# A mixture-of-experts stage: second blocks of up to 64 rows in two products instead of three, and weight splits spread over nine places

## The chip, the core and the metric

The kernel runs on one core of a Trainium2 chip. The metric is the device time of one execution in microseconds (us). A core has TensorE (PE, matrix products out of SBUF into PSUM, with PEld for its weight loads), VectorE (DVE), ScalarE (ACT), GpSimd (POOL) and SyncE (SP), and 16 DMA engines. The engines run side by side, each in the order of its own instructions, and wait for one another through semaphores.

## The reference

One encoder layer on 2048 tokens of width 1024, all in float32: windowed attention and a two-way mLSTM, gated and projected, and then a mixture of 32 experts, each token in two of them. The change is in the experts alone:

```python
xs = xt[row_tok].reshape(nblk, MOE_BLOCK, D)          # rows of an expert, in blocks of 128

def expert_block(args):
    xb, e = args
    return (jax.nn.silu(xb @ w_gate[e]) * (xb @ w_up[e])) @ w_down[e]

ys = lax.map(expert_block, (xs, blk_e)).reshape(P, D)
y = jnp.zeros((T, D), ys.dtype).at[row_tok].add(ys * row_w[:, None].astype(ys.dtype))
```

`w_gate` and `w_up` are 1024 x 512 and `w_down` 512 x 1024 for each expert, so an expert has 6.3 MB of weights. Counted with the reference's own routing on its inputs, the 32 experts get between 89 and 180 rows. 15 of them have more than 128: experts 1, 7, 8, 10, 11, 14 to 17, 19, 20 and 27 to 30. The fullest second block has 52 rows.

## The kernel before

Everything ahead of the experts (projections, attention, mLSTM, routing) is left alone by the change. The experts' stage is the end of `_body`, lines 1519 to 1776; its loop over the experts starts at line 1721.

**How a product keeps float32.** A float32 matrix is split into two parts that TensorE multiplies: `hi`, the rounded value (ACT writes it), and `lo`, what is left (a subtraction on DVE or POOL). A product x w is then three products into one PSUM bank: x_hi w_hi, x_lo w_hi, x_hi w_lo. Rows are the 128-column stationary side, weights the 512-column moving side.

**Weights.** An expert's weights are 12 pieces: 8 row blocks of gate and up (`raw`), 4 of down (`rawd`), two pieces to a loaded tile of 1 MB, six of these at a time (`NRAW`, SP issues the loads). `wsplit(n)` splits a piece: `ehi` on ACT (L1560), `elo` on DVE, or on POOL for the pieces in `POOL_J` (L1562). Split pieces lie in a ring of 14, so 2 pieces of the next expert can be split before this one is done. Where splits stand in each engine's order is set by hand, by `SPLITS`: six pieces at place 0 (the start of the expert), the others at four later places.

**A block.** `Block` does up to 128 rows. `head` makes 48 products with gate and up (L1615 with `ehi`, L1618 with `elo`; two halves of the columns, h = 0 and 1, with 24 each), silu and product of a half (L1627 on ACT, L1628 on DVE), transposes it (L1634) and splits it (L1635, L1636). The 24 products with down (L1644, L1645, L1649) are half in `head`, half in `tail`; then the result is scaled (`y`, L1703 on ACT, L1704 on DVE) and POOL adds it to the output rows with an indirect DMA (L1705). `xturn` transposes and splits the rows (L1589 on PE, L1590, L1591), for the next expert's block behind this one's `head`.

**Second blocks.** `nb` holds the number of blocks of each expert. In a branch at the top of the loop (L1725) POOL gathers the second block's 128 rows (`xgB`, L1726). In a branch behind the first block's `head` (L1745) a second `Block` does all of it again, 72 products in three passes, with no split of a weight between its products; without a second block only the first one's `tail` stands there. On the way without it, POOL makes up for the skipped DMA with a semaphore instruction (INC_SWDGE_SEM) in either branch.

Of the kernel before, what the change touches and what calls it, by code (L numbers as in the profile page):

```python
# [20 lines left out]
P = 128  # L21
S = 2048
# [18 lines left out]
def bucket_table():  # L41
    """Relative position to bucket, as one-hot rows, and the window's mask as a last row."""
# [12 lines left out]
class Chains:  # L55
    """Queues of generators, each advanced a step at a time between blocks of matrix products."""
# [55 lines left out]
def _body(tc, nc, A, out, scr_ext, upto, es):  # L112
# [68 lines left out]
    # gates of the mLSTM, all tokens: [i|f] x tile x (dir, head)  # L181
# [12 lines left out]
    def rstd(dst, ssq, n, cnt, scale=1.0):  # L194
        """scale * (ssq / cnt + eps) ** -0.5 on GpSimd, the scale a power of two"""
# [5 lines left out]
    PW = 272  # L201

    class Stream:
# [9 lines left out]
        def dma(self, n):  # L213
            """load half n % 2 of piece n // 2"""
# [70 lines left out]
    # order of the column pieces in a chunk of tokens  # L285
# [30 lines left out]
    def run_mms(mms, nsub=6):  # L316
        """mms: list of (out, lhsT, rhs, start, stop); chains advance between sub-blocks."""
# [11 lines left out]
    # ================= first half: projections, attention, forward mLSTM =================  # L329
# [19 lines left out]
    def small_loads():  # L349
# [7 lines left out]
        # per-channel vectors: conv taps (5), conv bias, merge biases, all halved  # L357
# [6 lines left out]
    def setup():  # L364
        """attention bias [query, head, key], per-channel columns, empty slots"""
# [26 lines left out]
        # a row of zeros past the tokens, weight 0  # L392
# [21 lines left out]
    # ---- rms norm and transposition of a tile of x  # L414
# [33 lines left out]
    # ---- attention  # L448
# [133 lines left out]
    # ---- mLSTM  # L582
    def gprep(c, d, seed=False):
        """stabiliser and decay of direction d for the tiles of chunk c"""
# [61 lines left out]
    def mload(t, d):  # L646
        """a tile's q and v; forward its k, backward what the forward pass left: k by rows and k q"""
# [15 lines left out]
    def mhead(n, t, d):  # L663
        """what a tile of the recurrence does without the state, at most a tile ahead of it"""
# [48 lines left out]
    def mtile(n, t, d):  # L713
        """one tile of the recurrence"""
# [71 lines left out]
    def mpost(n, t, h_):  # L786
        """both directions joined, normed and gated"""
# [32 lines left out]
    # ---- convolution over time, silu  # L820
# [17 lines left out]
    def conv_tail():  # L838
        """the last two tokens, with zeros behind them"""
# [957 lines left out]
```

## Time and profile before

| | |
|---|---|
| device time, 3 runs | median 2782.31 us (2769.46 to 2784.45) |
| span of the profiled execution | 2774.9 us |
| experts' stage, first to last product | 1784.8 to 2763.7 us of the span: 978.9 us |
| TensorE clock granted, whole span | 0.971 of full speed |
| second blocks executed | 15 |

The page gives the span of the profiled execution and no other time for it; it lies between the fastest run and the median. A row of the timeline has the start, the duration, the engine, the line, the operation, output <- input, how many were merged, and in brackets how long the engine was idle before it and what ended that. A product's duration includes the way through the array and overlaps the next one's, so the spacing of starts is what counts. Of a group of instructions the row has the busy time and mean duration in ns, and after the second bar the idle time before them with what ended it.

### The profile page before, as it was taken

To read this page: it belongs to the slowest core of one execution; us is meant where nothing else is said; L and a number is where in the kernel's file an instruction comes from. 1 tells how busy PE (TensorE), PEld (TensorE's weight loads), DVE (VectorE), ACT (ScalarE), POOL (GpSimd) and SP (SyncE) were. 2 spreads that over 40 slices of the span, in tenths; PEclk is the share of its full clock that TensorE was granted. 3 is DMA by queue.
4 is the path that set the end of the run, shared out by engine and by line. 5 is a ranking of instruction groups with operands and counts; after the bars stand their busy time and mean duration, and the time that the engine had idled before them with its cause. 6 is when DMAs were issued, how large, how long until landed. Compare 5 with 4: busy or idle time off the path is not lost. (4 is left out here: it accounts for less than half of the span.)

```text
span 2774.9 us, 39144 instructions
## 1 busy us (share of the span) xinstructions
PE 2562.3 (92%) x14112; PEld 2129.0 (77%) x14113; DVE 1556.6 (56%) x2537; ACT 1283.7 (46%) x2500; POOL 1243.0 (45%) x1029
## 2 busy tenths in 40 slices
PE   7999999999999999978998989799999999988997
PEld 6778977897789787757977878677777777766775
DVE  4454445454545645558594937667454544567544
ACT  4444545454445444433332422357553544556543
POOL 5444444244433442324444445357643543545433
PEclk9999999999999999989999999899999999999998
DMA  5534434453345345477765644679876876779763
GB/s 159 156 113 149 135 111 121 141 160 107 114 137 161 114 127 164 148 195 213 230 199 179 186 152 127 223 252 344 283 257 191 297 242 195 266 232 324 267 194 109
DMA packets 348967, 518.68 MB, mean 187 GB/s; under 512 B 24747, under 2 KB 212228, under 8 KB 348748
## 3 DMA queue, kind: packets, MB, share of 16 engines
q1 hardware_dynamic: 332140, 460.03, 50.9%
q0 software_dynamic: 15440, 51.60, 7.9%
q10 hardware_dynamic: 1168, 4.21, 0.4%
q8 instruction: 126, 2.06, 0.3%
q14 instruction: 93, 0.76, 0.1%
HBM read 420.30 MB, written 95.47 MB: 186 GB/s over the span
## 5 line engine op out<-in xcount | busy, mean ns | idle before, releaser
L239 POOL TENSOR_TENSOR wlo<-wraw,whi 128x512 fp32r<-128x512 f32 (+1 forms) x422 | 572.7, 1386 | 472.4 <-ACT whi L236 454.4
L1618 PE MATMUL mm<-elo,xhi 128*128 128x512 f32 x752 | 276.2, 419 | 87.1 <-DVE elo L1562 50.5
L1562 DVE TENSOR_TENSOR elo<-raw,ehi 128x1024 fp32r<-128x1024 f32 x192 | 297.2, 1589 | 39.8 <-ACT ehi L1560 36.0
L1615 PE MATMUL mm<-ehi,xhi 128*128 128x512 f32 x752 | 307.6, 409 | 0.0
L319 PE MATMUL mm<-hThi,whi 128*128 128x512 f32 x768 | 306.9, 400 | 0.0
L319 PE MATMUL mm<-hTlo,whi 128*128 128x512 f32 x768 | 304.4, 396 | 0.0
L319 PE MATMUL mm<-hThi,wlo 128*128 128x512 f32 x768 | 304.0, 396 | 0.0
L1615 PE MATMUL mm<-ehi,xlo 128*128 128x512 f32 x752 | 302.4, 402 | 1.3 <-issue 1.3
L236 ACT ACTIVATE whi<-wraw 128x512 fp32r<-128x512 f32 (+1 forms) x424 | 233.4, 622 | 136.9 <-PE mm L319 59.1
L319 PE MATMUL mm<-whi,hThi 128*128 128x256 f32 (+1 forms) x896 | 260.3, 291 | 3.9 <-ACT ev L898 1.8
L319 PE MATMUL mm<-wlo,hThi 128*128 128x256 f32 (+1 forms) x896 | 256.0, 286 | 1.1 <-POOL wlo L239 1.1
L319 PE MATMUL mm<-whi,hTlo 128*128 128x256 f32 (+1 forms) x896 | 255.8, 285 | 0.0
L1618 PEld LDWEIGHTS mm<-elo,xhi 128*128 128x128 f32 x752 | 146.9, 198 | 139.8 <-DVE elo L1562 64.3
L1560 ACT ACTIVATE ehi<-raw 128x1024 fp32r<-128x1024 f32 x256 | 253.0, 1048 | 1.7 <-issue 0.5
L1705 POOL DMA_INDIRECT out<-y,idx x47 | 102.3, 2176 | 263.4 <-ACT ehi L1560 237.9
L1562 POOL TENSOR_TENSOR elo<-raw,ehi 128x1024 fp32r<-128x1024 f32 x64 | 156.4, 2444 | 127.9 <-ACT ehi L1560 127.2
L1562 POOL TENSOR_TENSOR elo<-rawd,ehi 128x1024 fp32r<-128x1024 f32 x64 | 163.9, 2560 | 79.0 <-ACT ehi L1560 79.0
L319 PEld LDWEIGHTS mm<-whi,hThi 128*128 128x128 f32 x896 | 170.2, 190 | 7.9 <-ACT ev L898 2.1
L319 PEld LDWEIGHTS mm<-wlo,hThi 128*128 128x128 f32 x896 | 170.3, 190 | 3.6 <-issue 1.6
L1615 PEld LDWEIGHTS mm<-ehi,xlo 128*128 128x128 f32 x752 | 147.5, 196 | 30.5 <-DVE xlo L1591 0.4
L319 PEld LDWEIGHTS mm<-hThi,wlo 128*128 128x128 f32 x768 | 144.3, 188 | 34.0 <-issue 3.2
L319 PEld LDWEIGHTS mm<-whi,hTlo 128*128 128x128 f32 x896 | 170.0, 190 | 0.3 <-DVE hTlo L444 0.2
(421 smaller groups left out, 5872.6 us busy)
## 6 DMA issues: line engine op xcount, KB each, us to landing
wraw<-w_in SPq DMA_DIRECT2D x152, 512.0 KB
raw<-w_expert_gate SPq DMA_DIRECT2D x128, 512.0 KB
raw<-w_expert_up SPq DMA_DIRECT2D x128, 512.0 KB
rawd<-w_expert_down SPq DMA_DIRECT2D x64, 1024.0 KB
mg_s<-evg SPq DMA_DIRECT2D x64, 256.0 KB
gt<-mg_s SPq DMA_DIRECT2D x32, 512.0 KB
wraw<-w_out SPq DMA_DIRECT2D x32, 512.0 KB
xt<-x SPq DMA_DIRECT2D x16, 512.0 KB
```

Of the source, the lines that this page charges most:

```text
L236: nc.scalar.activation(hi[:, ks, :W], r[:, k:k + 2, :W], AF.Copy)
L239: eng.tensor_sub(lo[:, ks, :W], r[:, k:k + 2, :W], hi[:, ks, :W].bitcast(F32))
L319: nc.tensor.matmul(o, l, r, start=st, stop=sp)
L1560: nc.scalar.activation(dst[0], src, AF.Copy)
L1562: eng.tensor_tensor(dst[1], src, dst[0].bitcast(F32), op=OP.subtract)
L1615: nc.tensor.matmul(self.gu[h], x_[:, k, :], self.wt(k)[0][:, h, :], start=k == 0 and i == 0, stop=False)
L1618: nc.tensor.matmul(self.gu[h], self.xs[0][:, k, :], self.wt(k)[1][:, h, :], start=False, stop=stop)
L1705: nc.gpsimd.indirect_dma_start(out=out, out_offset=bass.IndirectOffsetOnAxis(ap=self.idx, axis=0), in_=y, in_offset=None, compute_op=OP.add)
```

## The change

- A second block of up to 64 rows goes to a new class `Small`. Its rows' two parts stand side by side as one stationary tile of 128 columns (`xs`: 64 of hi, 64 of lo), which is multiplied with `ehi` and with `elo` of each piece: 2 products where there were 3. Rows 0 to 63 of the sum are then the part of x_hi, rows 64 to 127 that of x_lo. `fold` adds the two halves by a product with `sel` (two identities over each other), which transposes at the same time; behind the product with down, ACT and DVE add the halves, POOL scales (L1734) and issues the indirect DMA (L1735).
- The second block is in two short branches in the middle of the first block: transposition and the products with gate and up between `begin` and `after` (L1791); fold and the products with down beside `end` (L1798).
- Its gather has 64 rows, stands outside any branch and is made for every expert, one expert ahead.
- The splits stand at nine places. Five pieces (before: two) are split ahead of an expert's first product; `POOL_J` is (2, 5, 8, 11) instead of (1, 5, 8, 10).
- The first block's gate and up products go by pairs of pieces and halves; the rows' parts are four tiles of half the depth, so that a product waits for its half.
- An expert with over 192 rows would have all blocks but the first in the loop at the end, with its weights loaded anew; `nb` and `two` are counted for that.

The rest of the diff takes out comments and renames helpers of `Block` (`head` is now `begin`, `middle`, `after`; `tail` is `end`).

```diff
-    nc.vector.tensor_scalar(nbf, cnt[0:1, :], 127.0, None, op0=OP.add)
+    nc.vector.tensor_scalar(nbf, cnt[0:1, :], 192.0, None, op0=OP.is_gt)
+    nc.vector.scalar_tensor_tensor(nbf, cnt[0:1, :], 127.0, nbf, op0=OP.add, op1=OP.mult)
...
         def up(self, h, k0, k1):
             for k in range(k0, k1):
-                self.up_x(h, k)
-                self.up_w(h, k, k == KT - 1)
+                for i, x_ in enumerate(self.xs[k // 4]):
+                    nc.tensor.matmul(self.gu[h], x_[:, k % 4, :], self.wt(k)[0][:, h, :],
+                                     start=k == 0 and i == 0, stop=False)
+            for k in range(k0, k1):
+                nc.tensor.matmul(self.gu[h], self.xs[k // 4][0][:, k % 4, :], self.wt(k)[1][:, h, :],
+                                 start=False, stop=k == KT - 1)
...
+        def begin(self, at):
+            for i, (h, k) in enumerate(((0, 0), (1, 0), (0, 2), (1, 2), (0, 4), (0, 6))):
+                at(f"p{i}")
+                self.up(h, k, k + 2)
+            self.room()
+            self.act(0)
+            at("a0")
+            self.a0 = self.a
+            self.turned()
+            self.room()
+        def middle(self):
+            self.up(1, 4, 7)
+            self.turn(0, self.a0)
+            self.up(1, 7, KT)
+            self.act(1)
+        def after(self, at):
+            at("a1")
+            self.down(0, (0, 1))
+            at("d0")
+            self.down(1, (0, 1))
+            at("d1")
+            self.turn(1, self.a)
+            at("t1")
...
+    class Small:
+        def __init__(self, wt, xg, idx_c, wgt_c):
+            self.wt, self.xg, self.idx, self.wgt = wt, xg, idx_c, wgt_c
+            self.xs = mo.tile([P, KT, 2, 64], F32R, name="xs")
+            self.hs = mo.tile([P, 4, 2, 64], F32R, name="hs")
+            self.g = mo.tile([P, 2, 512], F32, name="g")
+            self.a = mo.tile([P, 2, 2, 64], F32, name="sa")
+            self.p = mp.tile([P, KT, 64], F32, name="tr", bufs=2)
+            self.ps = [mp.tile([P, 512], F32, name="mm", tag=f"a{h}B") for h in range(2)]
+        def turn(self):
+            for k in range(KT):
+                nc.tensor.transpose(self.p[:, k, :], self.xg[0:64, k * P:(k + 1) * P], ident[0:64, 0:64])
+            nc.scalar.activation(self.xs[:, :, 0, :], self.p, AF.Copy)
+            nc.vector.tensor_sub(self.xs[:, :, 1, :], self.p, self.xs[:, :, 0, :].bitcast(F32))
+        def product(self, h, lhs, w, k, n):
+            for m in range(2):
+                nc.tensor.matmul(self.ps[h], lhs[:, k].rearrange("p a t -> p (a t)"), w[m][:, h, :],
+                                 start=k == 0 and m == 0, stop=k == n - 1 and m == 1)
+        def up(self):
+            for h in range(2):
+                for k in range(KT):
+                    self.product(h, self.xs, self.wt(k), k, KT)
+                if h == 0:
+                    nc.scalar.activation(self.g[:, 0, :], self.ps[0], AF.Copy)
+                else:
+                    nc.vector.tensor_copy(self.g[:, 1, :], self.ps[1])
+        def fold(self, h, room):
+            p = room[:, h].rearrange("p a (b t) -> p (a b) t", b=2)
+            for k in range(4):
+                nc.tensor.matmul(p[:, k, :], self.g[:, h, k * P:(k + 1) * P], sel, start=True, stop=True)
+            a = self.a[:, h]
+            nc.scalar.activation(a, p[:, 0:2], AF.Silu)
+            nc.vector.tensor_mul(a, a, p[:, 2:4])
+            hs = self.hs[:, 2 * h:2 * h + 2]
+            nc.scalar.activation(hs[:, :, 0, :], a, AF.Copy)
+            nc.vector.tensor_sub(hs[:, :, 1, :], a, hs[:, :, 0, :].bitcast(F32))
+        def down(self):
+            y = self.g[0:64].rearrange("p h f -> p (h f)")
+            for k in range(4):
+                for h in range(2):
+                    self.product(h, self.hs, self.wt(8 + k), k, 4)
+            for h in range(2):
+                cs = slice(512 * h, 512 * h + 512)
+                nc.scalar.activation(y[:, cs], self.ps[h][64:128, :], AF.Copy)
+                nc.vector.tensor_add(y[:, cs], self.ps[h][0:64, :], y[:, cs])
+            nc.gpsimd.tensor_scalar(y, y, self.wgt[0:64, :], None, op0=OP.mult)
+            nc.gpsimd.indirect_dma_start(out=out, out_offset=bass.IndirectOffsetOnAxis(ap=self.idx[0:64, :], axis=0),
+                                         in_=y, in_offset=None, compute_op=OP.add)
...
-    POOL_J = (1, 5, 8, 10)
-    SPLITS = {0: (2, 3, 4, 5, 6, 7), 1: (8,), 2: (9, 10), 3: (11,), 4: (12,)}
+    POOL_J = (2, 5, 8, 11)
+    FIRST = 5
+    SPLITS = {"p0": (5, 6), "p1": (7,), "p3": (8,), "p4": (9,), "p5": (10,), "a0": (11,), "a1": (12,),
+              "d1": (13, 14), "end": (15, 16)}
...
+    def gather_small(e):
+        t = mo.tile([P, D], F32, name="xgB")
+        nc.gpsimd.indirect_dma_start(out=t[0:64, :], out_offset=None, in_=h2_ap,
+                                     in_offset=bass.IndirectOffsetOnAxis(ap=idx[0:64, 32 + e:33 + e], axis=0))
+        return t
+    xgB = {0: gather_small(0)}
...
-    for n in range(RING - NPC):
+    two = mo.tile([1, 32], I32, name="two")
+    twof = mo.tile([1, 2, 32], F32, name="twof")
+    for i, n in enumerate((float(P), float(P + 64))):
+        nc.vector.tensor_scalar(twof[:, i], cnt[0:1, :], n, None, op0=OP.is_gt)
+    nc.vector.tensor_sub(two, twof[:, 0], twof[:, 1])
+    sel = mo.tile([P, 64], F32, name="sel")
+    for o in (0, 64):
+        nc.vector.tensor_copy(sel[o:o + 64, :], ident[o:o + 64, o:o + 64])
+    for n in range(FIRST):
         wsplit(n)
-    xsA = xtiles("")
-    for i in range(2):
-        xturn(xg[0], xsA, i, "")
+    xsA = [xturn(xg[0], i) for i in range(2)]
     for e in range(N_EXP):
-        v = nc.values_load(nb[:, e:e + 1], min_val=0, max_val=S // P)
-        nxt = {}
-        xgB = mo.tile([P, D], F32, name="xgB")
-        with tc.If(v > 1):
-            nc.gpsimd.indirect_dma_start(out=xgB, out_offset=None, in_=h2_ap,
-                                         in_offset=bass.IndirectOffsetOnAxis(ap=idx[:, 32 + e:33 + e], axis=0))
-        def between(i):
-            if i == 0 and e + 2 < N_EXP:
-                xg[e + 2] = gather(idx[:, e + 2:e + 3], "")
-            if i == 4 and held:
+        v = nc.values_load(two[:, e:e + 1], min_val=0, max_val=1)
+        w_e = lambda k, e=e: wts[NPC * e + k]
+        xsN = []
+        def at(place):
+            if place == "a1":
+                if e + 1 < N_EXP:
+                    xgB[e + 1] = gather_small(e + 1)
+                if e + 2 < N_EXP:
+                    xg[e + 2] = gather(idx[:, e + 2:e + 3], "")
+            if place == "d1" and held:
                 put(*held.pop(0))
-            for j in SPLITS.get(i, ()):
+            for j in SPLITS.get(place, ()):
                 wsplit(NPC * e + j)
-            if i == 4 and e + 1 < N_EXP:
-                nxt["x"] = xtiles("")
-                for h in range(2):
-                    xturn(xg[e + 1], nxt["x"], h, "")
-                wsplit(NPC * e + 13)
-        A_ = Block(lambda k: wts[NPC * e + k], xsA, idx[:, e:e + 1], wgt[:, e:e + 1], "")
-        A_.head(between)
-        xsA = nxt.get("x")
-        with tc.If(v > 1) as cmp:
-            xsB = xtiles("B")
-            A_.tail(lambda i: xturn(xgB, xsB, i, "B"))
-            B_ = Block(lambda k: wts[NPC * e + k], xsB, idx[:, 32 + e:33 + e], wgt[:, 32 + e:33 + e], "B", xgB)
-            B_.head()
-            B_.tail()
+            if place == "t1" and e + 1 < N_EXP:
+                xsN.extend(xturn(xg[e + 1], i) for i in range(2))
+        A_ = Block(w_e, xsA, idx[:, e:e + 1], wgt[:, e:e + 1])
+        B_ = Small(w_e, xgB[e], idx[:, 32 + e:33 + e], wgt[:, 32 + e:33 + e])
+        A_.begin(at)
+        with tc.If(v > 0) as cmp:
+            B_.turn()
+            A_.middle()
+            B_.up()
         with cmp.Else():
-            A_.tail()
-    # further blocks of experts with many rows
+            A_.middle()
+        A_.after(at)
+        with tc.If(v > 0) as cmp:
+            A_.end(lambda i: B_.fold(i, A_.p))
+            B_.down()
+        with cmp.Else():
+            A_.end()
+        at("end")
+        xsA = xsN
```

TensorE, inside the second block. Before, the last products with gate and up of a `Block`, the transposition of its activation, and its products with down (`xgB` serves as the room of the activation's parts there):

```order
L1634 MATMUL tr<-ident,ha 128x128 x2
L1615 MATMUL mm<-ehi,xhi 128x512
L1615 MATMUL mm<-ehi,xlo 128x512
L1618 MATMUL mm<-elo,xhi 128x512
L1644 MATMUL mm<-ehi,xgB 128x512
L1645 MATMUL mm<-elo,xgB 128x512
L1644 MATMUL mm<-ehi,xgB 128x512
L1645 MATMUL mm<-elo,xgB 128x512
L1649 MATMUL mm<-ehi,xgB 128x512 x2
```

Three products for each piece, two of them with `ehi`. TensorE in the second branch of the changed kernel, where the fold (L1717) stands between the first block's products and the second block's products with down follow:

```order
L1717 MATMUL th<-sel,g 128x64 x4
L1638 MATMUL mm<-ehi,hh 128x512
L1638 MATMUL mm<-elo,hh 128x512
L1638 MATMUL mm<-ehi,hh 128x512
L1638 MATMUL mm<-elo,hh 128x512
L1641 MATMUL mm<-ehi,hh 128x512 x2
L1701 MATMUL mm<-ehi,hs 128x512
L1701 MATMUL mm<-elo,hs 128x512
```

One product with `ehi` and one with `elo` now, and short products with `sel` ahead of them.

POOL, from the branches of one expert to those of the next, before (`nb`: number of blocks, read into a register; ISA: the semaphore instruction of the way without a second block):

```order
L1722 TENSOR_LOAD nb
L1725 COMPARE_AND_BRANCH
L1726 DMA xgB<-h_s,idx 128x1024
L1725 UNCONDITIONAL_BRANCH
L1725 ISA
L1725 UNCONDITIONAL_BRANCH
L1576 DMA xg<-h_s,idx 128x1024
L1562 TENSOR_TENSOR elo<-raw,ehi 128x1024
L1562 TENSOR_TENSOR elo<-rawd,ehi 128x1024 x2
L1562 TENSOR_TENSOR elo<-raw,ehi 128x1024
L1745 COMPARE_AND_BRANCH
L1705 DMA out<-y,idx 2176x1024 x2
```

The same stretch of POOL now:

```order
L1678 DMA out<-y,idx 2176x1024
L1798 ISA
L1798 UNCONDITIONAL_BRANCH
L1771 TENSOR_LOAD two
L1564 TENSOR_TENSOR elo<-raw,ehi 128x1024
L1564 TENSOR_TENSOR elo<-rawd,ehi 128x1024 x2
L1791 COMPARE_AND_BRANCH
L1791 UNCONDITIONAL_BRANCH x2
L1751 DMA xgB<-h_s,idx 64x1024
L1578 DMA xg<-h_s,idx 128x1024
L1564 TENSOR_TENSOR elo<-raw,ehi 128x1024
L1798 COMPARE_AND_BRANCH
```

Both gathers have moved from ahead of the expert's first split on POOL to behind the third. DVE, from the start of an expert to its first activation, before:

```order
L1722 TENSOR_LOAD nb
L1725 COMPARE_AND_BRANCH
L1725 UNCONDITIONAL_BRANCH x2
L1562 TENSOR_TENSOR elo<-raw,ehi 128x1024 x5
L1628 TENSOR_TENSOR ha<-ha,mm 128x256
```

DVE there now, with the two pieces of place "end" ahead of the load of the register:

```order
L1564 TENSOR_TENSOR elo<-raw,ehi 128x1024 x2
L1771 TENSOR_LOAD two
L1564 TENSOR_TENSOR elo<-raw,ehi 128x1024 x2
L1564 TENSOR_TENSOR elo<-rawd,ehi 128x1024 x2
L1621 TENSOR_TENSOR ha<-ha,mm 128x256
```

Of the five parts of gate and up in a row, four are left, two of them started ahead of the register's load, and two parts of down have come to this place.

## Rows read from the trace of the kernel before

**Rows 1.** Busy time by stretch: length, engines, clock granted, DMA share, GB/s.

```profile
core 0: us, PE busy (x) PEld busy (x) DVE busy (x) ACT busy (x) POOL busy (x), PEclk, DMA share, GB/s
1784.80:2763.70 978.90, 889.99 (x3948) 704.17 (x3948) 551.03 (x584) 521.16 (x712) 486.91 (x227) 0.96 0.76 252
2485.10:2509.00 23.90, 19.75 (x86) 15.39 (x85) 18.23 (x16) 14.68 (x20) 13.21 (x6) 0.93 0.90 307
2509.00:2529.50 20.50, 18.91 (x89) 14.88 (x87) 15.97 (x16) 15.29 (x20) 14.50 (x6) 1.00 0.90 296
```

**Rows 2.** Waits of PE in the experts' stage: us in total, times, longest.

```profile
PE mm L1618 <- DVE elo L1562: 50.5, 20, 4.2
PE mm L1618 <- POOL elo L1562: 36.1, 19, 2.2
```

**Rows 3.** Timeline of PE, expert 24, without a second block, transposition to transposition.

```profile
2508.98 1.03 PE L1589 MATMUL tr<-ident,xg 128*128 128x128 f32 x8
...
2521.47 0.50 PE L1618 MATMUL mm<-elo,xhi 128*128 128x512 f32 x1 [1.01 <-POOL elo L1562]
2522.55 0.50 PE L1618 MATMUL mm<-elo,xhi 128*128 128x512 f32 x1 [0.58 <-DVE elo L1562]
...
2528.92 1.32 PE L1589 MATMUL tr<-ident,xg 128*128 128x128 f32 x8
```

**Rows 4.** Timeline of PE, a second block and the next first block.

```profile
2637.62 1.03 PE L1589 MATMUL tr<-ident,xg 128*128 128x128 f32 x8
...
2669.33 0.73 PE L1618 MATMUL mm<-elo,xhi 128*128 128x512 f32 x2 [2.17 <-POOL elo L1562]
...
2675.94 1.17 PE L1589 MATMUL tr<-ident,xg 128*128 128x128 f32 x8
```

**Rows 5.** Timeline of PE: two products 31 apart, short products; a group of DVE.

```profile
1758.21 1.08 PE L1392 MATMUL mm<-fe,fh 128*128 128x64 f32 x8
...
1809.15 0.39 PE L1615 MATMUL mm<-ehi,xhi 128*128 128x512 f32 x1
...
1816.18 0.39 PE L1615 MATMUL mm<-ehi,xlo 128*128 128x512 f32 x1
...
L1628 DVE TENSOR_TENSOR ha<-ha,mm 128x256 f32<-128x256 f32 x94 | 39.6, 422 | 202.5 <-ACT ha L1627 202.5
```

**Rows 6.** POOL's indirect DMAs, and its semaphore instruction of skipped branches (ns).

```profile
L1705 POOL DMA_INDIRECT out<-y,idx x47 | 102.3, 2176 | 263.4 <-ACT ehi L1560 237.9 <-DVE y L1704 14.8 <-DVEq L1756 7.0
L1576 POOL DMA_INDIRECT xg<-h_s,idx x32 | 38.6, 1208 | 25.6 <-issue 9.1 <-DVE wgt L1497 8.0 <-DMA slot_s<-ent,si 4.7
L1726 POOL DMA_INDIRECT xgB<-h_s,idx x15 | 20.4, 1363 | 4.7 <-issue 4.7
...
L1725 POOLq INC_SWDGE_SEM  x17: 632/1080/1574, 1780.8 to 2743.1; - x17
```

**Rows 7.** Timeline of POOL, DVE and PE around one long wait, expert 23.

```profile
2493.44 1.17 POOL L1576 DMA_INDIRECT xg<-h_s,idx  x1 [0.52 <-issue]
2494.03 7.51 DVE L1562 TENSOR_TENSOR elo<-raw,ehi 128x1024 fp32r<-128x1024 f32 x2 [0.29 <-ACT ehi L1560]
2494.64 2.38 POOL L1562 TENSOR_TENSOR elo<-raw,ehi 128x1024 fp32r<-128x1024 f32 x1
2496.97 2.34 POOL L1562 TENSOR_TENSOR elo<-rawd,ehi 128x1024 fp32r<-128x1024 f32 x1
2500.45 1.93 PE L1618 MATMUL mm<-elo,xhi 128*128 128x512 f32 x3 [4.15 <-DVE elo L1562]
...
2503.78 1.23 DVE L1562 TENSOR_TENSOR elo<-rawd,ehi 128x1024 fp32r<-128x1024 f32 x1 [0.52 <-ACT ehi L1560]
```

**Rows 8.** TensorE's branch (ns, min/median/max), and the page's queue of instruction loads.

```profile
L1745 PEldq COMPARE_BRANCH  x47: 73/169/356, 1805.8 to 2758.8; - x47
...
q8 instruction: 126, 2.06, 0.3%
```

**Rows 9.** The stretch of the experts' stage with the busiest DMA, columns as in Rows 1.

```profile
2530.00:2554.00 24.00, 19.84 (x86) 15.36 (x84) 17.87 (x16) 14.44 (x20) 13.02 (x6) 0.93 1.03 361
```

More of the change, by code (lines that the diff above doesn't have):

```diff
@@ L1604, in __init__ @@
                                   for i in range(2))
-            self.y = mo.tile([P, D], F32, name="y", tag="y" + tag)
-            self.gu = [self.ps(h) for h in range(2)]
-        def ps(self, h):
-            if self.tag:
-                return mp.tile([P, 512], F32, name="mm", tag=f"a{h}" + self.tag)
-            return mp.tile([P, 512], F32, name="mm", tag="a", bufs=3)
-        def up_x(self, h, k):
-            for i, x_ in enumerate(self.xs):
-                nc.tensor.matmul(self.gu[h], x_[:, k, :], self.wt(k)[0][:, h, :], start=k == 0 and i == 0, stop=False)
@@ L1692, in tail @@
[L1692 to L1701 removed]
+            nc.scalar.activation(hhi[:, 2 * h:2 * h + 2, :], p, AF.Copy)
+            nc.vector.tensor_sub(hlo[:, 2 * h:2 * h + 2, :], p, hhi[:, 2 * h:2 * h + 2, :].bitcast(F32))
@@ new lines, in down @@
+        def down(self, h, ks):
+            if len(self.dn) == h:
+                self.dn.append(self.ps())
+            for k in ks:
+                for w_ in self.wt(8 + k):
+                    nc.tensor.matmul(self.dn[h], self.hhi[:, k, :], w_[:, h, :],
+                                     start=k == 0 and w_ is self.wt(8)[0], stop=False)
+            for k in ks:
+                nc.tensor.matmul(self.dn[h], self.hlo[:, k, :], self.wt(8 + k)[0][:, h, :], start=False, stop=k == 3)
+        def begin(self, at):
[8 more added lines that the diff above has]
+            self.room()
@@ new lines, in middle, with end @@
+        def middle(self):
[11 more added lines that the diff above has]
+            at("t1")
+        def end(self, between=lambda i: None):
+            between(0)
+            self.down(0, (2, 3))
+            between(1)
+            self.down(1, (2, 3))
@@ L1764, in _body @@
                 g = gather(ix, "")
-                xs = xtiles("")
-                for h in range(2):
-                    xturn(g, xs, h, "")
+                xs = [xturn(g, h) for h in range(2)]
                 wt = {}
@@ L1772, in _body @@
                         wt[n] = split(r, n)
-                G = Block(wt.get, xs, ix, en[:, 1:2], "")
-                G.head()
-                G.tail()
+                G = Block(wt.get, xs, ix, en[:, 1:2])
+                G.begin(lambda place: None)
+                G.middle()
+                G.after(lambda place: None)
+                G.end()
 _INS = ["x", "norm1_g", "w_in", "attn_q_gain", "attn_k_gain", "attn_sink", "rel_bias_table",
```

107 lines of the change are left out of this document (22 added, 85 removed).

## The prediction

> **What bounds the kernel now.** I read the busy times by stretch first, then TensorE's waits, then its timeline. The change touches only the experts' stage, which takes 978.9 of the span's 2774.9 us [rows 1]. TensorE is busy for 890 us of it; no other engine reaches 60%, and the DMA share is 0.76. So the stage is bound by TensorE's own products and by what they wait for. What they wait for is one thing: the `lo` parts of the weights, 50.5 us for DVE's and 36.1 us for POOL's, 86.6 us together [rows 2]. No product waits for a weight's load or for rows.
>
> Now split the stage into clean work and waits. An expert without a second block takes 2528.92 - 2508.98 = 19.94 us from one transposition to the next, 1.01 + 0.58 of it waits [rows 3]: 18.35 us clean. A second block with the next first block takes 2675.94 - 2637.62 = 38.32 us, 2.17 of it a wait [rows 4]: 36.15 clean, so 17.80 us for the second block. Both stretches are experts at full clock or nearly so. With 32 first and 15 second blocks (47 results written, 15 second gathers [rows 6]) the clean work is 32 x 18.35 + 15 x 17.80 = 854.2 us. That leaves 978.9 - 854.2 = 124.7 us: the 86.6 of recorded waits and 38.1 of other time, mostly a clock that falls behind a long wait: the granted share is 0.93 in the 23.90 us of expert 23 and 1.00 in the next one [rows 1].
>
> **The second block in two products.** 72 products of 512 columns become 2 x 24 = 48. Two starts 31 products apart lie 1816.18 - 1809.15 = 7.03 us apart [rows 5], 0.227 us each. 24 fewer are 5.44 us. The short work around them: twelve transpositions go (eight of rows, four of the activation), eight with half the columns and eight folds come. Eight full transpositions take at most 1.03 us [rows 3], so what goes is up to 1.5. Eight short products of 128 x 64 take at most 1.08 us [rows 5], the nearest row for the folds; the half transpositions lie between half of 1.03 and 1.03. Net between 0.9 gained (folds near nothing) and 0.6 lost when all are counted in full; with transpositions that overlap, up to 1.1 lost. I take 0.4 lost, near the upper rows, because the folds and their operands are of the row's shape. So 5.0 us for each block, bounds 4.3 and 6.4, and for 15 blocks 75 us, bounds 65 and 97. Nothing hides or cancels this: the products are on TensorE, in its order, and the stage is bound there.
>
> What the second block hands to other engines lies beside products. Its two copies of the sums and the parts of its rows are made while the first block's twelve remaining gate and up products run (12 x 0.227 = 2.7 us). The fold's chain is four short operations, some 0.42 us each by DVE's 128 x 256 one [rows 5], 1.7 us, against six products between the last fold and the first that needs any of it and eight more before its own half is needed (14 x 0.227 = 3.2 us). If that cover were gone it would cost 15 x 1.7 = 25 us. Two branches per expert stay two; TensorE's takes 169 ns in its sequencer [rows 8] and no product in rows 2 waits for one.
>
> **The waits for `lo` parts.** POOL first. Before, ahead of its first split of an expert (piece 5), POOL had the previous result's DMA, semaphore instructions of 1.08 us or a second gather of 1.36, and a gather of 1.21 [rows 6]. Both gathers move behind the third split, and one of the two semaphore instructions goes. Piece 5 can start 1.08 + 1.21 = 2.3 us earlier without a second block and 1.36 + 1.21 = 2.6 us earlier with one. But its `lo` part is now wanted as product 30 of the expert instead of 35, 5 x 0.227 = 1.1 us earlier. So the waits of 2.17 us [rows 4] should fall to 0.7, those near 1.0 [rows 3] to nothing: 15 x 0.7 = 11 us. Against it, after a second block POOL has to scale 64 x 1024 elements ahead of the second result's DMA. No row shows that; it costs between nothing and the 2.4 us of a 128 x 1024 subtraction [rows 7], and I take 0.8, as one of the two inputs is missing and products 1 to 29 cover part: 12 us. Together 23 us, where there were 36.
>
> DVE next. Its long waits come from one pattern. A subtraction on DVE began at 2494.03 while POOL's gather was running; POOL's two subtractions followed at 2494.64 and 2496.97, and DVE's two pieces took 7.51 us, where one alone takes 1.23 [rows 7]. TensorE then waited 4.15 us, at a lower clock afterwards. DVE and POOL evidently do not subtract at the same time. The change takes away the gather at this place and shortens DVE's row from five pieces to four with two of them early, but pieces 5 and 8 can still follow each other on POOL. I take 28 us of the 50.5, a little over half, and no better reason than that one of the pattern's two parts is gone. The 38.1 us of other time go with the waits: 38.1 x 51/86.6 = 22. For waits of a new kind (POOL's second result, parts of the second block behind a split on ACT or DVE) I put 12 us, 0.8 for each second block; the trace before has no row for them.
>
> The trace shows that a piece on DVE waits for POOL's. The Trainium skill (SBUF — State Buffer, "SBUF: two separate sides") says that VectorE with two SBUF inputs and GpSimd share a pair of ports under an exclusive lock, and that whichever starts first has it for the whole instruction. The trace agrees on the lock and not on who wins: in rows 7 DVE's piece began 0.61 us ahead of POOL's and still was behind both. The rule speaks against the spreading: wherever splits stand, an expert's eight DVE pieces and four POOL pieces stay in one line. By rows that is 8 x 1.23 + 4 x 2.4 = 19.4 us, 1.1 more than a first block's clean 18.35. By that rule alone the seventeen experts without a second block wait 1.1 us each, 18 us in all, and the others not at all.
>
> **The sum.** 854.2 - 75 = 779 us clean; waits 23 + 28 + 22 + 12 = 85; the stage 864 instead of 978.9, a gain of 115. The start and the end of the span are unchanged: the first product waits for the first gather as before, and the three more pieces split there fit into that wait. The span of the profiled execution lies 7.4 us below the median of the runs; I take the time around the span as unchanged and subtract from the median: 2782.3 - 115 = **2668 us**. For the edges: waits of 25 us with the middle gain of the products give 2782.3 - (124.7 - 25) - 75 = 2608; waits of 165 us with the smallest gain of 65 give 2782.3 + 40 - 65 = 2757.
>
> **Rivals.**
> - *The waits stay as they are* (124.7 us). For it: the subtractions are the same number and DVE and POOL still exclude each other. Against it: POOL's first split comes earlier. 2782.3 - 75 = 2707 us.
> - *The waits all but go.* 779 + 25 us instead of 978.9: 2608 us. For it: five pieces are ready at the expert's first product, where there were two. Against it: 19.4 us of subtractions in 18.35 us of products.
> - *The loads become the bound.* The busiest stretch moved 361 GB/s at a DMA share of 1.03 in 24.00 us [rows 9], that is 8.7 MB, with loads ahead for the next expert. An expert without a second block needs its 6.3 MB of weights, two gathers and a result, some 7.6 MB, 21 us at that rate. Only the two runs of five and six such experts (2 to 6, 21 to 26) could feel it: 11 x (21 - 18.35) = 29 us of waits, which mostly replaces waits already in the sum; on top of it all, 2697 us.
> - *Taken branches cost.* The page counts 126 instruction loads on one queue, 0.3% of 16 x 2774.9 us [rows 8], 1.06 us each. If each of two jumps per expert stopped TensorE for one, 64 x 1.06 = 68 us: 2736 us. Against it: the kernel before jumps as often and no wait in rows 2 is for it. The Trainium skill (Runtime: NRT & Kernel Launch, "Instruction fetch mechanics") says that a taken branch out of the loaded window stops the engine until the target's page is there. No wait of the trace shows that here.
> - *Slower.* DVE's pattern of rows 7 twice in each expert: pieces 15 and 16 now stand behind the result's evacuation, beside POOL's DMA, and are wanted early in the next expert. Each time costs 4.15 us and the clock behind it about 1: 32 x 2 x 5.15 = 330 us of waits, 779 + 330 = 1109, 2912 us. It decides from 124.7 + 75 + 14 = 214 us of waits, 6.7 us per expert, where there are 3.9 now.
> - *It does not do what it says:* an expert with over 192 rows would load its weights again. The counts exclude it: the fullest has 180.
>
> **How the numbers follow.** Forecast 0.52 (2640 to 2695, with the loads' rival inside or just above); waits as now 0.24; waits gone 0.09; branches or an exposed fold 0.08; slower 0.03; and 0.04 for a gain that is lost in some new wait to within 0.5%, which is about what a measurement of this kernel can tell from no change. The range is 2612 to 2738: it takes in the waits as now and the branches, and leaves out the far edge of the waits gone, no change and slower. Faster 0.93, same 0.04, slower 0.03.
>
> **What would show it.** Right: 720 products with rows' and activation's parts of second blocks, in place of 1080; a second block with the next first block at 33 to 34 us from transposition to transposition; TensorE's waits for `lo` parts near 50 us and none for the fold. Wrong: an expert without a second block over 22 us; a DVE piece over 6 us in more than a third of the experts; waits of TensorE for `hs`, for `g` or for loads.

## The result

The change makes the kernel slightly slower, where the forecast was 115 us faster: a median of 2795.75 us (2792.43 to 2801.46, 5 runs) against 2781.38 us (2769.46 to 2784.45, 5 runs) of before, a ratio of 1.0068 (95% interval 1.0047 to 1.0089).

The profiled execution has a span of 2796.9 us, 22.0 more than before. Of these, 5.5 us are no work of the changed code: the experts' stage begins 5.5 us later, and the router's last rows ahead of it already stand 6.5 us later. The stage takes 993.7 us, where it took 978.9 [rows 1]. Its row in the view of busy times by stretch (columns as in [rows 1]):

```profile
1790.30:2784.00 993.70, 862.88 (x3763) 679.88 (x3764) 652.63 (x596) 514.23 (x723) 557.36 (x261) 0.92 0.77 245
```

TensorE does have less to do, 863 us in place of 890, but its granted clock fell from 0.96 to 0.92, and DVE and POOL are busy for 652.6 and 557.4 us, where it was 551.0 and 486.9. TensorE's waits in the changed kernel (total us, times, longest), to hold against [rows 2]:

```profile
PE mm L1613 <- POOL elo L1564: 65.2, 17, 4.6
PE th L1629 <- DVE ha L1621: 27.8, 8, 4.2
PE mm L1613 <- DVE elo L1564: 18.8, 16, 2.0
PE th L1717 <- DVE hh L1631: 17.6, 15, 1.5
```

There were 86.6 us of waits for `lo` parts. Now there are 84.0 for `lo` parts, and 45.4 more of a new kind: for the activation (`ha`, and its `lo` part in `hh`) that DVE computes.

To compare kernels I split the stage of each by the starts of TensorE's products, from the first product with gate to the last start. Idle time of TensorE that the profile puts down to another engine or to a DMA is a wait. Where two starts lie 0.33 to 0.47 us apart without a wait, what goes beyond 0.2285 us is put down to the lower clock. The rest is clean work; it also holds delays too short to be recorded as waits. In us:

| | before | forecast | after |
|---|---|---|---|
| clean work | 857 | 779 | 811 |
| waits | 89 | 63 | 131 |
| lower clock | 31 | 22 | 52 |
| stage | 977 | 864 | 993 |

So the clean work fell by 47 us and not by 75, and waits with the clock behind them rose by 63 where they were to fall by 35. An expert with a second block takes 39.5 us on average (39.4 before), one without 23.5 (22.7 before).

Where the waits come from is seen in two places of the timeline. First expert 5, which has no second block and none ahead of it; DVE, POOL and TensorE's wait (start, duration, operation, how many merged, idle before):

```profile
1929.60 4.58 DVE L1564 TENSOR_TENSOR elo<-raw,ehi 128x1024 fp32r<-128x1024 f32 x2 [0.17 <-ACT ehi L1562]
1929.86 3.24 POOL L1564 TENSOR_TENSOR elo<-raw,ehi 128x1024 fp32r<-128x1024 f32 x1
1933.05 6.67 POOL L1564 TENSOR_TENSOR elo<-rawd,ehi 128x1024 fp32r<-128x1024 f32 x2
1934.10 6.70 DVE L1564 TENSOR_TENSOR elo<-rawd,ehi 128x1024 fp32r<-128x1024 f32 x2
1940.73 0.41 DVE L1621 TENSOR_TENSOR ha<-ha,mm 128x256 f32<-128x256 f32 x1
1941.28 0.66 PE L1629 MATMUL th<-ident,ha 128*128 128x128 f32 x2 [4.16 <-DVE ha L1621]
```

Two parts that take 2.4 us alone take DVE 6.70 us while POOL works through its own. The activation stands behind them on DVE, and TensorE behind the activation. Second, the start of expert 18, behind a second block:

```profile
2366.01 2.36 DVE L1564 TENSOR_TENSOR elo<-raw,ehi 128x1024 fp32r<-128x1024 f32 x2 [0.16 <-ACT ehi L1562]
2366.03 4.98 POOL L1734 TENSOR_SCALAR g<-g,wgt 64x1024 f32<-64x1024 f32 x1 [2.30 <-DVE g L1733]
...
2371.29 1.56 POOL L1735 DMA_INDIRECT out<-g,idx  x1 [0.28 <-POOL g L1734]
2371.69 6.94 DVE L1564 TENSOR_TENSOR elo<-rawd,ehi 128x1024 fp32r<-128x1024 f32 x2 [0.21 <-ACT ehi L1562]
2372.36 2.86 POOL L1564 TENSOR_TENSOR elo<-raw,ehi 128x1024 fp32r<-128x1024 f32 x1
...
2375.28 0.80 PE L1613 MATMUL mm<-elo,xhi 128*128 128x512 f32 x1 [4.26 <-POOL elo L1564]
```

POOL's scaling and DMA stand ahead of its first subtraction, which the products want. The groups of the stage (busy time, mean in ns):

```profile
L1564 DVE TENSOR_TENSOR elo<-raw,ehi 128x1024 fp32r<-128x1024 f32 x192 | 314.3, 1678 | 21.9 <-ACT ehi L1562 21.7
L1564 DVE TENSOR_TENSOR elo<-rawd,ehi 128x1024 fp32r<-128x1024 f32 x64 | 175.8, 2786 | 5.6 <-ACT ehi L1562 5.5 <-issue 0.2
L1734 POOL TENSOR_SCALAR g<-g,wgt 64x1024 f32<-64x1024 f32 x15 | 74.6, 4971 | 35.0 <-DVE g L1733 35.0
L1717 PE MATMUL th<-sel,g 128*128 128x64 f32 x240 | 31.1, 273 | 17.6 <-DVE hh L1631 17.6
```

DVE's parts of down take 2.79 us on average, where one alone takes 1.23 [rows 7]. By single records, 63 of DVE's 256 parts take over 2 us, where it was 19.

### The profile page after: what moved, and what is told of

Read it like the earlier page. It is cut to its first block, busy times and chain, and to the rows that moved or that the text cites. A ratio compares the mean times of both kernels' runs of the same rounds, so it can differ in the third digit from the quotient of the medians.

```text
span 2796.9 us, 39211 instructions
## 1 busy us (share of the span) xinstructions
PE 2541.1 (91%) x13932; PEld 2109.3 (75%) x13933; DVE 1658.4 (59%) x2558; ACT 1279.1 (46%) x2515; POOL 1312.3 (47%) x1061
## 5 line engine op out<-in xcount | busy, mean ns | idle before, releaser
L1564 DVE TENSOR_TENSOR elo<-raw,ehi 128x1024 fp32r<-128x1024 f32 x192 | 314.3, 1678 | 21.9 <-ACT ehi L1562 21.7
L1613 PE MATMUL mm<-elo,xhi 128*128 128x512 f32 x512 | 186.6, 437 | 84.7 <-POOL elo L1564 65.2
L1564 POOL TENSOR_TENSOR elo<-raw,ehi 128x1024 fp32r<-128x1024 f32 x64 | 172.6, 2696 | 120.2 <-ACT ehi L1562 101.2
L1610 PE MATMUL mm<-ehi,xhi 128*128 128x512 f32 x512 | 225.8, 441 | 0.0
L1610 PE MATMUL mm<-ehi,xlo 128*128 128x512 f32 x512 | 220.3, 430 | 0.0
L1564 POOL TENSOR_TENSOR elo<-rawd,ehi 128x1024 fp32r<-128x1024 f32 x64 | 171.3, 2676 | 78.1 <-ACT ehi L1562 77.7
L1613 PEld LDWEIGHTS mm<-elo,xhi 128*128 128x128 f32 x512 | 107.0, 209 | 126.5 <-POOL elo L1564 76.8
L1564 DVE TENSOR_TENSOR elo<-rawd,ehi 128x1024 fp32r<-128x1024 f32 x64 | 175.8, 2786 | 5.6 <-ACT ehi L1562 5.5
L319 PEld LDWEIGHTS mm<-hThi,whi 128*128 128x128 f32 x768 | 144.6, 188 | 29.3
```

The lines of the kernel that those rows point to most:

```text
L319: nc.tensor.matmul(o, l, r, start=st, stop=sp)
L1564: eng.tensor_tensor(dst[1], src, dst[0].bitcast(F32), op=OP.subtract)
L1610: nc.tensor.matmul(self.gu[h], x_[:, k % 4, :], self.wt(k)[0][:, h, :], start=k == 0 and i == 0, stop=False)
L1613: nc.tensor.matmul(self.gu[h], self.xs[k // 4][0][:, k % 4, :], self.wt(k)[1][:, h, :], start=False, stop=k == KT - 1)
```

## The experiments

Two theories stood against each other. **A:** one new piece of work, POOL's scaling of the second result, delays POOL's parts. **B:** DVE and POOL exclude each other wherever their subtractions meet, so that every move of them only moves the wait. Beside them stood whether the saved products were saved at all, and whether the new places are at fault. In the diffs below, "after" is the changed kernel. All times are medians of 4 runs, with the ratio to the kernel before on the same chip (7 runs, medians 2777 to 2781 us). The versions ran on four chips, so a difference between two versions is good to some 3 us.

**Scaling moved off POOL.**

```diff
-            nc.gpsimd.tensor_scalar(y, y, self.wgt[0:64, :], None, op0=OP.mult)
+            nc.scalar.activation(y[:, 0:512], y[:, 0:512], AF.Copy, scale=self.wgt[0:64, :])
+            nc.vector.tensor_scalar(y[:, 512:], y[:, 512:], self.wgt[0:64, :], None, op0=OP.mult)
```

> The changed kernel with the second block's result scaled on ACT (first 512 columns) and DVE (last 512) instead of POOL, where the scaling took 4.97 us in each of 15 blocks. Theory A (POOL's scaling delays piece 2, the first piece that POOL splits): the 13 waits of about 4.3 us for POOL's `elo` behind a second block go, with about 1.5 us of slow clock behind each; 13 x 5.8 = 75 us, 2721 us. Theory B (DVE and POOL hold each other up wherever their subtractions meet): the wait only changes its name, to `ha` or DVE's `elo` with 2.1 to 4.2 us as in the experts behind one without a second block; a gain of 0 to 13 x 2.2 = 29 us, 2767 to 2796 us.

Measured: 2797.65 us, 1.0062 (1.0040 to 1.0083): nothing gained. TensorE's waits:

```profile
PE mm L1613 <- DVE elo L1564: 47.8, 41, 2.0
PE th L1629 <- DVE ha L1621: 36.4, 10, 4.2
PE mm L1613 <- POOL elo L1564: 23.1, 16, 1.7
PE th L1717 <- DVE hh L1631: 17.6, 15, 1.5
PE mm L1610 <- ACT g L1734: 5.4, 15, 0.6
```

The wait for POOL fell from 65.2 to 23.1 us, and those for DVE's parts and for `ha` rose from 46.6 to 84.2. Theory A falls as an account of the loss: the scaling was the last in the row, and without it the wait ended on DVE.

**A third product in the second block.**

```diff
-            for m in range(2):
+            for i, m in enumerate((0, 0, 1)):
```

> The changed kernel with the product with ehi made twice in the second block (it leaves the result wrong): 72 products of 512 columns again, all else as changed. If the stage follows TensorE's products, 15 x 24 x 0.227 = 82 us more: 2878 us. If the saved products had only been turned into waits for `lo` parts, most of the 82 us disappears in shorter waits: 2796 to 2835 us.

Measured: 2832.19 us, 1.0197 (1.0170 to 1.0224), 36 us above the changed kernel. Clean work rises by 79 us, as the products say, and waits and clock fall by 46 (131 + 52 to 101 + 36). So the products were saved, and more than half of what they saved went into longer waits.

**The old places under the new second block.**

```diff
-    POOL_J = (2, 5, 8, 11)
-    FIRST = 5
+    POOL_J = (1, 5, 8, 10)
+    FIRST = 2
...
+    SPLITS = {"p0": (2, 3, 4, 5, 6, 7), "p4": (8,), "a0": (9, 10), "a1": (11,), "t1": (12,)}
...
                 xsN.extend(xturn(xg[e + 1], i) for i in range(2))
+                wsplit(NPC * e + 13)
```

> The changed kernel's two-product second block with the places of before: two pieces split ahead, POOL's pieces 1, 5, 8, 10, six pieces at the expert's start. If the spreading of the splits is what took the gain, TensorE's waits go back to the 2.3 and 3.2 us per expert of before and about 55 to 75 us are gained on before: 2710 to 2730 us. If POOL's scaling is the main cause, it now stands ahead of piece 5 and TensorE still waits over 4 us behind each second block: 2770 to 2810 us.

Measured: 2822.66 us, 1.0145 (1.0120 to 1.0171), worse than the changed kernel. Neither case came as expected: waits stay at 133 us, but most of them are for DVE and not for POOL (POOLq is POOL's sequencer, here at the second branch):

```profile
PE mm L1613 <- DVE elo L1564: 88.1, 58, 2.8
PE mm L1613 <- POOL elo L1564: 17.8, 16, 3.0
PE mm L1613 <- POOLq L1798: 15.7, 15, 1.3
```

The spreading is not what took the gain. That this version is slower than the changed kernel shows in the other two terms, clean work of 837 us in place of 811 and a lower clock of 59 in place of 52.

**No subtraction on POOL.**

```diff
-    POOL_J = (2, 5, 8, 11)
+    POOL_J = ()
```

> The changed kernel with no subtraction on POOL: all twelve `lo` parts on DVE, the scaling left on POOL. If the two engines' lock is the cause (DVE's 256 parts took 500 us instead of 256 x 1.22 = 312), twelve parts take 12 x 1.22 = 14.7 us of DVE per expert and no part takes over 2 us; waits fall below 2 us in most experts: 2680 to 2720 us. If DVE is simply short of time (14.7 plus some 5 us of other work in 18.5 to 19 us of products), TensorE waits 2 us or more for DVE in every expert without a second block: 2760 to 2850 us.

Measured: 2664.25 us, 0.9576 (0.9552 to 0.9599): 131 us faster than the changed kernel, by giving one engine the work of two. DVE's parts and TensorE's waits:

```profile
L1564 DVE TENSOR_TENSOR elo<-raw,ehi 128x1024 fp32r<-128x1024 f32 x256 | 309.2, 1267 | 20.1 <-ACT ehi L1562 19.3 <-issue 0.5
L1564 DVE TENSOR_TENSOR elo<-rawd,ehi 128x1024 fp32r<-128x1024 f32 x128 | 150.9, 1214 | 7.9 <-ACT ehi L1562 7.9
```

```profile
PE th L1629 <- DVE ha L1621: 15.7, 18, 2.4
PE th L1717 <- ACT xhi L1588: 11.8, 15, 0.8
PE mm L1638 <- ACT hh L1630: 7.7, 6, 4.5
PE mm L1701 <- DVE xs L1697: 5.6, 11, 0.5
```

384 parts on DVE keep it busy for 460 us; 256 took 490 beside POOL. The stage splits into 799 clean, 49 of waits and 16 of clock, 864 us. This version beats both kernels. The edit takes away two things at once: POOL's hold on DVE, and products that wait for a part of POOL's own, which takes 2.4 us and more where one on DVE takes 1.2. How the 131 us divide between them is not shown; the run with one part left on POOL, below, has the hold alone. The longest waits of this version are in runs of experts without a second block, where ACT waits for the weights' loads:

```profile
ACT ehi L1562 <- DMA rawd<-w_expert_down: 14.8, 16, 2.3
ACT ehi L1562 <- DMA raw<-w_expert_up: 12.7, 10, 4.0
```

**The same in the kernel before.** `POOL_J = ()` in place of `(1, 5, 8, 10)`.

> The kernel before with no subtraction on POOL, all else as before. If the lock between DVE and POOL costs the kernel before too (86.6 us of waits for `lo` parts and some 29 us of slow clock), most of it goes: 2690 to 2720 us, and then moving the subtractions gains more than the whole change does. If only the changed kernel's nine places make the two engines meet badly, little comes of it, and six DVE parts in a row at the start of an expert (6 x 1.22 = 7.3 us) bring waits of their own: 2770 to 2810 us.

Measured: 2688.83 us, 0.9672 (0.9655 to 0.9688). POOL's subtractions cost the kernel before, too, and one line there brings 89 us without the rest of the change. Its stage is 848 clean, 24 waits, 13 clock. The wait for `lo` that had been 86.6 us:

```profile
PE mm L1618 <- DVE elo L1562: 12.0, 30, 0.4
```

**Third product, scaling and old places again, without POOL's subtractions.** The edits are those above, on top of `POOL_J = ()`.

> No subtraction on POOL as in e4, and the product with ehi made twice in the second block (it leaves the result wrong). With the lock out of the way the 24 products should cost their full time: 15 x 24 x 0.227 = 82 us on top of 2664, 2746 us. If waits still pace the second block (1.6 us per expert are left, 0.8 of it ahead of the fold), 15 x 1.6 = 24 us of it are hidden: 2722 us.

Measured: 2751.82 us, 0.9902 (0.9878 to 0.9926), 88 us above the version without POOL's subtractions: the 24 products cost their full time, 5.8 us for each block, and none of it is hidden.

> e4 with the second block's scaling moved from POOL to ACT and DVE as in e1; nothing but DMAs is left on POOL. If POOL's scaling matters only through what stands behind it on POOL (now no subtraction, only DMAs), it changes nothing: 2660 to 2668 us. If ACT's and DVE's time is what is short at the start of an expert, it costs the 0.3 us for ACT that e1 showed and some 0.3 us for DVE behind each of 15 blocks, up to 10 us: 2675 us.

Measured: 2664.55 us, 0.9595 (0.9579 to 0.9611), the same as with the scaling on POOL. Where it stands makes no difference.

> e4 with the places of before as in e3 (two pieces split ahead, six at the expert's start). If the places matter by themselves, six DVE parts at the start (7.3 us) against products that want a new piece every 6 x 0.227 = 1.4 us bring back waits of 1 to 3 us per expert: 2700 to 2740 us. If they mattered only through the lock, the time is that of e4: 2655 to 2675 us.

Measured: 2708.66 us, 0.9755 (0.9739 to 0.9772), 44 us slower than with the new places, and only in part for the reason that I had expected. The six parts at the start cost some 20 us (8 of waits for `elo`, and 12 of starts of two `elo` products that lie further apart). The second block's short chain, late behind DVE, costs 18 by its rows below, 35.4 us in place of 17.4; the 15.7 of waits for `ha` are gone. The lower clock costs 37 us, where it was 16:

```profile
PE th L1717 <- DVE sa L1720: 24.8, 15, 1.7
PE mm L1613 <- DVE elo L1564: 12.4, 32, 0.6
PE mm L1701 <- DVE xs L1697: 10.6, 15, 2.6
```

The pairs of runs together, in us:

| | subtractions on DVE and POOL | on DVE alone |
|---|---|---|
| before | 2777 | 2689 |
| after | 2796 | 2664 |
| after, three products | 2832 | 2752 |
| after, old places | 2823 | 2709 |

**One piece left on POOL.** `POOL_J = (11,)`.

> The changed kernel with one of the four subtractions left on POOL, piece 11, the others on DVE. If each part on POOL costs about the same, a quarter of the 132 us between the changed kernel and e4 comes back: 2697 us. If what costs is POOL's parts in a row (DVE gets no turn between them), one part by itself costs at most one hold of 2.4 - 1.2 us per expert off TensorE's path: 2660 to 2675 us.

Measured: 2704.76 us, 0.9735 (0.9719 to 0.9751). One part per expert costs 40 of the 131 us, so it does not take several of them behind one another. TensorE never waits for POOL here. Beside POOL's one part (2.4 us) 15 of DVE's parts take 3.4 us in place of 1.2, and it is again the activation behind them that comes late, where 15.7 us of such waits had been without it:

```profile
PE th L1629 <- DVE ha L1621: 54.6, 21, 3.4
```

**Copies on POOL in place of subtractions.**

```diff
-        eng = nc.gpsimd if j in POOL_J else nc.vector
-        eng.tensor_tensor(dst[1], src, dst[0].bitcast(F32), op=OP.subtract)
+        if j in POOL_J:
+            nc.gpsimd.tensor_copy(dst[1], src)
+        else:
+            nc.vector.tensor_tensor(dst[1], src, dst[0].bitcast(F32), op=OP.subtract)
```

> The changed kernel with POOL's four subtractions replaced by copies of the same size from the loaded tile (one input instead of two; it leaves the result wrong). If only instructions of POOL with two inputs hold DVE up, DVE's parts take 1.22 us again and the time is near e4's: 2665 to 2690 us. If every instruction of POOL holds DVE for as long as it runs, DVE's parts are still held but for less time, and over a third of the 132 us stays: 2710 us or more.

Measured: 2695.92 us, 0.9717 (0.9694 to 0.9740), between the two: 24% of the 131 us stay.

```profile
L1566 DVE TENSOR_TENSOR elo<-raw,ehi 128x1024 fp32r<-128x1024 f32 x192 | 261.8, 1404 | 25.3 <-ACT ehi L1562 22.1 <-issue 2.1
L1566 DVE TENSOR_TENSOR elo<-rawd,ehi 128x1024 fp32r<-128x1024 f32 x64 | 122.6, 1948 | 17.0 <-ACT ehi L1562 16.7
L1564 POOL CAST elo<-rawd 128x1024 fp32r<-128x1024 f32 x64 | 90.0, 1465 | 24.5 <-DMA rawd<-w_expert_down 22.8 <-PE mm L1615 1.7
```

POOL's instruction with one input holds DVE up as well, only for less time: DVE's parts of down take 1.95 us, not 1.22, and 4.1 us where it meets three copies in a row. But this hold is not what the 24% are: TensorE waits for `ha` less than without any part on POOL (9.6 us, 15.7 there), and the new wait is for POOL's own first copy, behind the scaling, once in each of 15 blocks:

```profile
PE mm L1615 <- POOL elo L1564: 43.4, 15, 3.2
```

The test is not a clean one either, since a copy does not wait for ACT's `hi` part and so runs at other times. The Trainium skill (SBUF — State Buffer, "SBUF: two separate sides") has the engine that starts second blocked for the whole instruction of the other, where VectorE has two inputs in SBUF and GpSimd's instruction reads SBUF. The hold by a copy agrees with that.

**Folds and places moved**, on top of `POOL_J = ()`: both folds behind six products, pieces 9 and 10 a place later.

```diff
-            A_.end(lambda i: B_.fold(i, A_.p))
+            A_.end(lambda i: i and [B_.fold(h, A_.p) for h in range(2)])
...
-    SPLITS = {"p0": (5, 6), "p1": (7,), "p3": (8,), "p4": (9,), "p5": (10,), "a0": (11,), "a1": (12,),
+    SPLITS = {"p0": (5, 6), "p1": (7,), "p3": (8,), "p5": (9,), "a0": (10, 11), "a1": (12,),
```

> e4 (all parts on DVE) with both folds behind the first six products of the second branch instead of one ahead of them, and pieces 9 and 10 split one place later, so that the first activation is ahead of piece 10 on DVE. If the waits that e4 still shows (0.8 us per second block ahead of the fold, 0.4 to 1.2 us for `ha`) go without a new one, 12 + 16 us are gained: 2636 us. If the fold's chain is then late for the products with down (1.7 us against 6 products, 1.4 us), 15 x 0.3 us of it come back, and if loads bound the runs of experts without a second block, `ha`'s share does not come: 2650 to 2665 us.

Measured: 2661.80 us, 0.9578 (0.9562 to 0.9595), the same as without it. The waits for `xhi` and `ha` went, and others of the same size came, 49 us in both:

```profile
PE mm L1701 <- DVE xs L1697: 15.9, 15, 2.8
PE mm L1638 <- ACT hh L1630: 15.0, 7, 4.8
PE th L1717 <- DVE sa L1720: 11.1, 15, 0.7
```

**The folds made twice**, on top of `POOL_J = ()`.

```diff
-                nc.tensor.matmul(p[:, k, :], self.g[:, h, k * P:(k + 1) * P], sel, start=True, stop=True)
+                for _ in range(2):
+                    nc.tensor.matmul(p[:, k, :], self.g[:, h, k * P:(k + 1) * P], sel, start=True, stop=True)
```

> e4 with each of the eight short products of the folds made twice (same result). It prices the term of the sum that was put at nearly nothing. If the eight products are the eight of the row that the prediction took for them (1.08 us at most), 15 x 1.0 = 15 us more: 2679 us. If, as the trace's 16 records for 8 products say, they take 2 x 0.9 us on TensorE's path, 15 x 1.8 = 27 us more, 2691 us, and up to 8 us beyond that if the fold's chain becomes late for the products with down.

Measured: 2693.68 us, 0.9694 (0.9678 to 0.9711), 29 us above the version with the folds once. Clean work rises from 799 to 826 us, 1.81 us for each second block.

```profile
L1718 PE MATMUL th<-sel,g 128*128 128x64 f32 x480 | 57.9, 274 | 11.8 <-ACT xhi L1588 11.8
```

## Why the prediction was wrong

- **What bounds the kernel now: right as far as it went.** The clean work of before, 854 us by two stretches, is 857 by all of them. That the waits were for `lo` parts was right. That they had one cause, the subtractions on POOL, was not drawn as a conclusion: without them the kernel before loses 65 of its 89 us of waits and 17 of its 31 us of slow clock.
- **The 24 products: right.** 0.227 us each, 5.44 for a block; the third product costs 5.3 us of clean work in one run and 5.8 us of time in the other. They came off: 720 products stand in place of 1080.
- **The short work: the term was mis-sized.** I put it at 0.4 us lost for each block, at most 1.1. The row behind its upper bound was misread: its eight records are four products, two records each (the source makes four in a row there), so eight such products stand for 2.16 us and not 1.08. The eight of the folds take 1.81 us, in 16 records (240 in 15 blocks). With 1.81 for them the same sum gives 0.8 to 1.3 us lost for each block, 6 to 14 us more over 15 blocks than had been allowed, of the 28 missing between 75 and 47.
- **The products themselves: put at the same 0.227 us in both kernels, without a check.** Where two products of 512 columns follow each other at full clock (starts 0.20 to 0.26 us apart), the mean distance is 0.2282 us before and 0.2327 in the changed kernel, and 0.2325 to 0.2327 in every version of it above; without POOL's subtractions the kernel before keeps 0.2287. Over 3024 products that is, by estimate, 13 us more of the 28. What in the new order causes it no run shows.
- **POOL's wait: wrong in size, and it was the wrong thing to size.** The scaling was bounded by 2.4 us and taken as 0.8; it stood for 4.97 us, above the upper end (2.85 where no subtraction of DVE was under way at its start, see the end). POOL's wait became 65.2 us in place of 23. But taking the scaling off POOL gained nothing, so that correcting this term would not have saved the forecast.
- **DVE's wait: the step that failed.** I took 28 of 50.5 us "as one of the pattern's two parts is gone". That treated the pattern of [rows 7] as one meeting, which moves could take apart. The runs show that the two engines hold each other up wherever their subtractions meet: twelve parts spread over the expert meet at other places, and hold up other things. Waits for DVE are 64.2 us (18.8 + 27.8 + 17.6), some 70% of them for the activation behind the parts, which no row of before had shown waiting. My 12 us for waits of a new kind were 45. Without POOL's subtractions, all else unchanged, the waits for DVE's weight parts and for `ha` are 20 us (4.3 + 15.7).
- **The clock** went with the waits, as forecast, but upwards: 52 us in place of 22.
- **The lock's rule.** By the line of 19.4 us of subtractions in 18.35 us of products I had put its price at 18 us. The line assumes that the parts are packed and that none is wanted before its turn. Measured, POOL's four parts cost 131 us, the waits for POOL's own parts among them.
- **The rivals.** The mechanism of the slower case was the right one, DVE held up by POOL anew in each expert, but its price of 330 us was too high and so its chance of 0.03 too low. I had put the point from which it decides at 214 us of waits, 14 of them to be clear of no change; with clean work down by only 47 us it lies at 89 + 31 + 47 + 14 = 181, and 183 came. At 0.7% slower, what came lies next to the case with the chance of 0.04, a gain lost in new waits, for which I had named no mechanism. The loads did not bind here; they show only in the version at 2664 us. Of exposed branches there is no wait in the changed kernel; the fold waits, 1.2 us a block, for `hh`.
- **What would show it.** Of the signs of "right" only the 720 products came: an expert with a second block takes 39.5 us and not 33 to 34, and the waits for `lo` parts are 84 us and not 50. The first sign of "wrong" came, 23.5 us for an expert without a second block, but it was badly chosen: the average was 22.7, over the limit of 22, before the change. My 19.94 us were of one of the quickest experts, 20.3 by the same measure as the averages; such experts took 20.2 to 25.2. The second did not come: 8 parts of DVE took over 6 us, though 24 took over 5, where it was 10. Nor did the third as written: TensorE's waits are for `ha` and `hh`, which the list did not have, and not for `hs`, `g` or loads.

The stage that I had forecast, 864 us, is the one measured without POOL's subtractions. This agrees only in the sum: its clean work is 20 us above the forecast and its waits and clock 20 below.

## What to carry to other kernels

When two engines exclude each other, ask first whether the second one should have any of this work: four of twelve parts moved from POOL to DVE brought 131 us here, and 89 in the kernel before, although DVE then does all of it. A wait that ends on such a pair is not removed by moving one party; its name changes, as the scaling's did. And a change that takes work off the bound engine should be priced with that pair alone as the limit, because what it saves may turn into longer waits, as 46 of 79 us did here.

## What was not expected of the hardware

- A DVE subtraction of 128 x 1024 takes 1.22 us with nothing but DMAs on POOL, and up to 6.3 us beside POOL's in single records of the changed kernel. POOL's parts are lengthened as well, from 2.44 and 2.56 us before to 2.70 and 2.68.
- POOL's scaling of 64 x 1024 is recorded with 4.97 us, and the same 4.98 with no subtraction on POOL at all. Each time two DVE subtractions run at their normal 1.2 us from its start on, and the third takes 2.06 us in that version. With the old places, with POOL's subtractions and without them, DVE has none under way when the scaling starts, in all 15 blocks, and it is recorded with 2.85 us. So at least 2.1 of the 4.97 us go with DVE's subtractions. No run priced the scaling with DVE idle throughout, so its own time stays open.
- A product of the fold (128 x 64, both operands plain float32) leaves two records and takes 0.23 us, as much as one of 512 columns (0.227).
